# The border between the mixer and the cross-attention: first weights begun before the second token tile's norm, low parts of the query weights in other places, two groups' wide products in a row

## The chip, the cores and the metric

The kernel runs on one core of one Trainium2 chip. Times are device microseconds (us) of one execution; a kernel's time is the median of several runs. The engines named below are PE (TensorE: matmuls, with PEld for its weight loads), DVE (VectorE: elementwise work, 32x32 block transposes), ACT (ScalarE: copies, casts, activations), POOL (GpSimd) and SP (SyncE, which here only issues DMAs).

## What is computed

Two layers, each of four blocks with a residual sum and a layer norm: a SwiGLU, the mixer, the cross-attention, a second SwiGLU. 256 tokens of width 1024, 256 memory rows, everything in float32. What matters here is the end of the mixer and the start of the cross-attention:

```python
def layer_norm(x, g, b):
    xf = x.astype(jnp.float32)
    mu = jnp.mean(xf, axis=-1, keepdims=True)
    var = jnp.mean(jnp.square(xf - mu), axis=-1, keepdims=True)
    return ((xf - mu) * lax.rsqrt(var + LN_EPS)).astype(x.dtype) * g + b
...
    q = (x @ wq).reshape(bsz, s, CA_HEADS, CA_HEAD_DIM)
    k = (mem @ wk).reshape(bsz, m, CA_HEADS, CA_HEAD_DIM)
    v = (mem @ wv).reshape(bsz, m, CA_HEADS, CA_HEAD_DIM)
...
        mix = jnp.concatenate([y_conv, y_rec, y_pool], axis=-1) @ w_out[l]
        h = layer_norm(ALPHA * h + mix, ln_g[l, 1], ln_b[l, 1])
        h = layer_norm(ALPHA * h + cross_attn(h, mem, ca_q[l], ca_k[l], ca_v[l], ca_o[l]),
                       ln_g[l, 2], ln_b[l, 2])
```

The values (`mem @ wv`) don't depend on the norm; the queries (`x @ wq`) need all of it.

## The kernel before

**Split numbers.** Each matmul operand is held as a rounded high part and a low part. `split` (L74 to L77) makes them: ACT casts the high part (L75), DVE subtracts it from the source (L76, recorded in the list `lows`). A product is high times high, high times low and low times high. In `mm_cols`, which forms 128 output columns for all 256 tokens, a *wide* product takes one high 128x128 block of a weight against a token block with high and low part side by side (512 columns), and a *narrow* one takes the low block of the weight against the high part alone (256 columns). It issues seven wide products, eight narrow ones and the last wide one, into one PSUM bank. Weights of 512 columns come in four tiles of two row blocks each: so product k of a chain needs tile k // 2.

**Weights.** `load` issues the DMAs on SP into `raw` tiles (6 buffers), and splits them into `whi` and `wlo` tiles (8 buffers of each). With `hold` it only lists the splits in `todo`, and the caller issues them.

**Tokens.** They lie in two tiles of 128, `h[0]` and `h[1]`. `project_back` multiplies the mixer's output with `w_out` in four slabs of two row blocks; the last three slabs are run for one token tile and column half at a time (`tail`), so that each tile can be normed as soon as its sums are done. `finish` norms: `tile_done(i)` adds the sums to `h[i]` (L378), makes the mean (DVE, L388), the square on ACT (L393), the variance (DVE, L399), its power on POOL (L405) and two more DVE passes (L408, L413, the latter recorded in `normed`).

**The border.** With `across` set (this border alone), after `tile_done(0)` four DMAs on POOL's queue deal `h[0]` out to the tile `dealt` (L424), `tile_done(1)` follows, and two DVE transposes (L433) make `turned` from `dealt`: the first tile's tokens, turned. In `attention`, `values` loads `ca_v` (512 columns) and forms the values of the memory rows; these products, 24 for each of two row tiles, keep PE busy while the norm ends. Within the second row tile's products, `first_rows` splits `turned` into `xT` (before k = 0), and `pend` turns the second token tile with eight PE transposes into two PSUM banks and splits these into the other half of `xT` (before k = 4). Then `query(0)` loads `ca_q` and forms the queries of two heads in two pairs of column groups; `query(1)` does so for the next columns. Banks: `acc` tiles have four PSUM banks in common, and the values' two sums, the two turned banks and the queries' sums all come from these four.

**Order.** Tile's planner sets the order on each engine at build time, from the order in the program and its own estimate of what is ready when; it fills an engine's wait with later work that is ready. `with tc.issue_after(ins)` puts what a block issues on the engine of `ins` behind `ins`, and does nothing on the other engines. Before the change, `ca_q`'s low parts for both halves were put behind the last norm pass in this way (`normed[-1]`). Once built, the list of each engine is fixed.

Of the kernel before, what the change touches and what calls it, by code (L numbers as in the profile page):

```python
# [17 lines left out]
P = 128  # L18
# [42 lines left out]
def model(ctx: ExitStack, tc: tile.TileContext, t: dict, out: bass.AP):  # L61
# [79 lines left out]
    def mm_cols(w, cols, x):  # L141
        o = acc()
        for k in range(NK - 1):
            product(o, w.at(k, cols)[0], x[:, k], k == 0, False)
        for k in range(NK):
            product(o[:, 0, :], w.at(k, cols)[1], x[:, k, 0, :], False, False)
        product(o, w.at(NK - 1, cols)[0], x[:, NK - 1], False, True)
        return sums(o)

    def add(dst, o):  # L150
        dst = dst if len(dst.shape) == 3 else halves(dst)
# [177 lines left out]
    def finish(mm, y, scale, gb, units, last=False, junk=None, ahead=None, prompt=False, across=None):  # L329
# [25 lines left out]
        def tile_done(i):  # L355

            st = sm.tile([P, 4, 6], F32, tag="st", name="st")
            pieces, size = [slice(0, 512), slice(512, DM)], 512
            if last and i == NT - 1:

                pieces, size = [slice(0, 512), slice(512, 768), slice(768, DM)], 256
                c = slice(512, DM)
                v = halves(h[i][:, c])
                with tc.issue_after(lows[-1].ins):
                    nc.vector.scalar_tensor_tensor(v, v, ALPHA / scale, sums(y[i][1]), op0=ALU.mult, op1=ALU.add)
            for c in pieces:
                n = c.start // 512
                v = halves(h[i][:, c])
                if len(pieces) == 3 and n:
                    o = acc((P, 256))  # L370
                    mm(i, n, slice(c.start - 512, c.stop - 512), o, None)
                    nc.vector.tensor_tensor(v, v, sums(o), op=ALU.add)
                else:
                    mm(
                        i, n, slice(0, 512), None,
                        None if last or across or not i or not n else turn_first,
                    )
                    nc.vector.scalar_tensor_tensor(  # L378
                        v, v, ALPHA / scale, sums(y[i][n]), op0=ALU.mult, op1=ALU.add,
                        accum_out=None if junk is None else st[:, n, 0:1],  # L380
                    )
                for d in range(c.start, c.stop, size):
                    if junk is None:
                        nc.vector.bn_stats(st[:, d // size, :], h[i][:, d : d + size])
            mv = sm.tile([P, 2], F32, tag="mv", name="mv")
            rs = sm.tile([P, 1], F32, tag="rs", name="rs")
            if junk is not None:
                mean = nc.vector.tensor_scalar(  # L388
                    mv[:, 0:1], st[:, 0, 0:1], st[:, 1, 0:1], -1.0 / DM, op0=ALU.add, op1=ALU.mult
                )  # L390
                with ExitStack() as behind:
                    squared.append(
                        nc.scalar.activation(junk, h[i], AF.Square, bias=mv[:, 0:1], accum_out=mv[:, 1:2])  # L393
                    )
                    if prompt:
                        with tc.issue_after(mean.ins):
                            low_part(held.pop(0))
                        behind.enter_context(tc.issue_after(lows[-1].ins))
                    nc.vector.tensor_scalar(  # L399
                        rs, mv[:, 1:2], 1.0 / DM, LN_EPS / scale / scale, op0=ALU.mult, op1=ALU.add  # L400
                    )
            else:
                nc.vector.bn_aggr(mv, st[:, 0 : DM // size, :])
                nc.vector.tensor_scalar_add(rs, mv[:, 1:2], LN_EPS / scale / scale)
            nc.gpsimd.tensor_tensor(rs, rs, nhalf[:, 0:1], op=ALU.pow)  # L405
            cs = [slice(0, 512), slice(512, DM)]
            for c in cs:
                nc.vector.scalar_tensor_tensor(  # L408
                    h[i][:, c], h[i][:, c], mv[:, 0:1], g[:, c],
                    op0=ALU.subtract if junk is None else ALU.add, op1=ALU.mult,  # L410
                )
            for c in pieces:
                normed.append(nc.vector.scalar_tensor_tensor(  # L413
                    h[i][:, c], h[i][:, c], rs, b[:, c], op0=ALU.mult, op1=ALU.add
                ))
                if last:
                    e = nc.scalar if c.start == 512 else nc.sync
                    e.dma_start(out[0, tok(i), c], h[i][:, c])

        if across is not None:  # L420
            tile_done(0)
            x = across()
            for a in range(4):
                dealt = nc.gpsimd.dma_start(  # L424
                    x[a * 32 : a * 32 + 32].rearrange("p (b c) -> p b c", b=4), h[0][:, a * 256 : (a + 1) * 256]
                )
            with tc.issue_after(dealt.ins):
                tile_done(1)
            o = wp.tile([P, DM], F32, tag="lng", name="turned").rearrange("p (k t) -> p k t", k=NK)
            m = x.rearrange("p (b j k) -> p k b j", b=4, k=NK)  # L430
            with tc.issue_after(normed[-1].ins):
                for d in (slice(0, 4), slice(4, 8)):
                    nc.vector.transpose(o[:, d].rearrange("p k (r b) -> p k b r", b=4), m[:, d])  # L433
            firsts.append(o)
        elif ahead is None:
            tile_done(0)
            tile_done(1)
        else:
            split(*ahead.todo[0])
            if prompt:  # L440
                nc.scalar.copy(ahead.todo[1][0], ahead.todo[1][2])
                held.append(ahead.todo[1])
            with tc.issue_after(lows[-1].ins):
                tile_done(0)
            with tc.issue_after(normed[-1].ins):
                if prompt:
                    split(*ahead.todo[2])
                    split(*ahead.todo[3])
                tile_done(1)
                if not prompt:  # L450
                    for x in ahead.todo[1:]:
                        split(*x)
            if prompt:
                with tc.issue_after(normed[-1].ins):
                    low_part(held.pop())
# [500 lines left out]
            d = slice(4 * c + 2 * p, 4 * c + 2 * p + 2)  # L956
            split(kTh[:, d, :], kTl[:, d, :], o)

    def values(l, c, vh, vl, between={}):
        w = load(t["ca_v"][l], 0, NK, c * CHUNK, CHUNK, across=True)  # L960
        for i in range(NT):
            o = acc((P, 512))
            for k in range(NK):
                if k % 2 == 0:
                    between.get(4 * i + k // 2, lambda: None)()
                wh, wl = w.at(k, slice(0, CHUNK))
                mm_rows(o, mT[:, k, 0, tok(i)], mT[:, k, 1, tok(i)], wh, wl, k == 0, k == NK - 1)
            d = slice(c * CHUNK, (c + 1) * CHUNK)
            split(halves(vh[:, i, d]), halves(vl[:, i, d]), sums(o))

    def mixer(l, fill):
        w_in = t["w_in"][l]
        with tc.tile_pool(name="mix", bufs=1, reuse_waits="tile") as mp:

# [336 lines left out]
            def slab(a):  # L1313
# [2 lines left out]
            return project_back(  # L1316
                [slab(a) for a in (0, 6, 2, 4)], 3, gb, 1.0, idn,
                junk=v.rearrange("p i c -> p (i c)"),
                across=lambda: mp.tile([P, DM], F32, tag="q", name="dealt"),
            )  # L1320


    def attention(l, pend):
        scale = (DM // HEADS) ** -0.5
        with tc.tile_pool(name="att", bufs=1, reuse_waits="tile") as ap:
            qTh = ap.tile([P, NK, SEQ], F32R, name="qTh")
# [4 lines left out]

            def query(c, between=None):

                with tc.issue_after(normed[-1].ins):
                    w = load(t["ca_q"][l], 0, NK, c * CHUNK, CHUNK, across=True)
                for p in range(2):
                    o = sm.tile([P, 2, SEQ], F32, tag="sums", name="sums", bufs=1)
                    for j in range(2):
                        add(o[:, j, :], mm_cols(w, slice((2 * p + j) * P, (2 * p + j + 1) * P), xT))
                    d = slice(4 * c + 2 * p, 4 * c + 2 * p + 2)  # L1340
                    split(qTh[:, d, :], qTl[:, d, :], o)
                    if between is not None and p == 0:
                        between()
# [68 lines left out]

            def first_rows():
                for d in (slice(0, 4), slice(4, 8)):
                    split(xTh[:, d, tok(0)], xTl[:, d, tok(0)], firsts[-1][:, d])

            pT = []
            values(l, 0, vh, vl, {4: first_rows, 6: pend})
            query(0)
            gb = ln_params(l, 2)  # L1420
            query(1, lambda: (weights(0), deal(0), weights(1), deal(1)))
# [25 lines left out]
    for l in range(DEPTH):  # L1447
# [2 lines left out]
            following=(lambda: key_weights(l, 0, True)) if l else None,  # L1450
        )
        keys(l, 0, {6: pend}, started)
        pend = mixer(l, lambda: keys(l, 1))
        pend = attention(l, pend)
        end = l == DEPTH - 1
        started, pend = ffn(
            l, "ffn2", 3, pend, last=end,
# [29 lines left out]
```

## Time and profile before

| | |
|---|---|
| median of 3 runs (lowest, highest) | 1065.58 us (1065.34, 1065.7) |
| the profiled execution, its own time | 1064.91 us |
| its span, first to last instruction | 1063.2 us |
| PE busy / DVE busy / ACT busy / POOL busy | 99% / 88% / 63% / 9% of the span |
| granted TensorE clock, mean | 0.999 |
| instructions | 16487 |

The border is passed twice, once in each layer: at about 281 to 306 us and at about 805 to 830 us of the span. In the rows of the timeline, the first two numbers are start and length in us, then come engine, line, operation, what is written from what, and the count of instructions merged in the row; brackets at the end hold the engine's idle time before the row and what ended it. The length of a merged row reaches from its first start to its last end.

### The profile page before, as it was taken

The page shows a single profiled execution, that of the slowest core. Times are in us where ns is not written, and L with a number is a line of the kernel's source. Part 1 is how long each engine was busy: PE and PEld are TensorE (multiplying, and loading weights), DVE is VectorE, ACT ScalarE, POOL GpSimd, SP SyncE. Part 2 cuts the span into 40 slices and gives each one's busy share as a digit, 9 for nine tenths or more (in the row PEclk, how much of TensorE's full clock was granted, in tenths as well). Part 3 has the DMA queues.
Part 4 walks back from the last instruction along what each step waited for, and adds up shares of the span by engine and source line. Part 5 has one row for each costly group of instructions (what it writes and reads, how often), then busy time and mean ns, then how long its engine had stood idle before and what let it go on. Part 6 is the DMA issues. An engine that isn't in the chain of part 4 may idle for free.

```text
span 1063.2 us, 16487 instructions
## 1 busy us (share of the span) xinstructions
PE 1050.1 (99%) x5998; PEld 932.8 (88%) x5998; DVE 932.6 (88%) x1250; ACT 666.8 (63%) x917; POOL 99.6 (9%) x136
## 2 busy tenths in 40 slices
PE   9999999999999999999999999999999999999997
PEld 7888888989889888889888888898998898888896
DVE  6998898989899789897898987999898887898888
ACT  6675775676657557655665656666775665675661
POOL 8002001000100001010001001010001000000001
PEclk9999999999999999999999999999999999999999
DMA  9999984754775589988789987866636765799862
GB/s 362 298 318 281 262 267 164 254 166 150 228 249 193 168 283 231 358 200 215 242 304 258 337 226 203 271 232 221 209 117 212 258 234 173 242 283 310 234 201 70
DMA packets 142689, 252.11 MB, mean 237 GB/s; under 512 B 11376, under 2 KB 52112, under 8 KB 142608
## 3 DMA queue, kind: packets, MB, share of 16 engines
q1 hardware_dynamic: 130656, 228.89, 65.0%
q0 software_dynamic: 11376, 20.99, 11.1%
q10 hardware_dynamic: 576, 1.18, 0.3%
q8 instruction: 47, 0.77, 0.3%
q14 instruction: 34, 0.28, 0.1%
HBM read 234.50 MB, written 1.05 MB: 222 GB/s over the span
## 4 chain that ended last, share of the span: by engine, by line
PE 92%; DVE 4%; DMA 1%; issue 1%; ACT 1%; POOL 0%; DVEq 0%; ACTq 0%; POOLq 0%; SPq 0%
PE acc L132 61%; PE dn L132 28%; DVE wlo L76 2%; ACT whi L75 1%; PE acc L200 1%; DMA h<-in_x_dram 1%; DMA dealt<-h 1%; DVE turned L433 0%; PE dn L1155 0%; DMA raw<-in_ca_q_dram 0%; PE dn L1229 0%; DVE h L413 0%; DVE raw L718 0%; DVE h L408 0%; DVE al L76 0%
## 5 line engine op out<-in xcount | busy, mean ns | idle before, releaser
L76 DVE TENSOR_TENSOR wlo<-raw,whi 128x1024 fp32r<-128x1024 f32 (+1 forms) x452 | 534.3, 1209 | 51.9 <-ACT whi L75 47.2
L75 ACT CAST whi<-raw 128x1024 fp32r<-128x1024 f32 (+1 forms) x452 | 455.9, 1042 | 186.8 <-PE acc L132 47.0
L132 PE MATMUL acc<-whi,xT 128*128 128x512 f32 (+1 forms) x1064 | 313.7, 372 | 0.0
L132 PEld LDWEIGHTS acc<-whi,xT 128*128 128x128 f32 x1064 | 199.1, 189 | 26.7
L132 PE MATMUL acc<-wlo,xT 128*128 128x512 f32 (+1 forms) x532 | 197.9, 372 | 0.0
L132 PE MATMUL dn<-whi,ah 128*128 128x512 f32 x346 | 131.5, 380 | 0.0
L132 PE MATMUL dn<-wlo,ah 128*128 128x512 f32 x346 | 131.2, 379 | 0.1
L132 PE MATMUL dn<-whi,al 128*128 128x512 f32 x346 | 131.1, 379 | 0.0
L132 PE MATMUL acc<-xT,whi 128*128 128x512 f32 x480 | 118.2, 382 | 3.3 <-DVE xT L76 3.3
L132 PEld LDWEIGHTS acc<-wlo,xT 128*128 128x128 f32 x532 | 100.6, 189 | 13.3
L132 PEld LDWEIGHTS acc<-xT,whi 128*128 128x128 f32 x480 | 86.5, 190 | 13.6 <-DVE xT L76 4.1
L132 PE MATMUL dn<-whi,xT 128*128 128x512 f32 x288 | 87.3, 380 | 0.0
L132 PEld LDWEIGHTS dn<-wlo,ah 128*128 128x128 f32 x346 | 65.4, 189 | 9.4 <-DVE wlo L76 0.5
L132 PEld LDWEIGHTS dn<-whi,al 128*128 128x128 f32 x346 | 65.4, 189 | 9.3
L132 PEld LDWEIGHTS dn<-whi,ah 128*128 128x128 f32 x346 | 65.4, 189 | 9.0
L132 PEld LDWEIGHTS acc<-xT,wlo 128*128 128x128 f32 x480 | 63.1, 191 | 4.1 <-DVE wlo L76 0.9
L132 PE MATMUL acc<-xT,wlo 128*128 128x256 f32 x480 | 63.8, 275 | 0.1
L132 PE MATMUL acc<-wlo,kTh 128*128 128x512 f32 (+1 forms) x176 | 61.7, 351 | 0.0
L132 PE MATMUL acc<-whi,kTl 128*128 128x512 f32 (+1 forms) x176 | 61.7, 351 | 0.0
L132 PE MATMUL acc<-whi,kTh 128*128 128x512 f32 (+1 forms) x176 | 61.7, 351 | 0.0
L132 PEld LDWEIGHTS dn<-whi,xT 128*128 128x128 f32 x288 | 54.4, 189 | 7.7 <-DVE xT L76 0.2
L132 PE MATMUL dn<-wlo,xT 128*128 128x512 f32 x144 | 54.6, 379 | 0.0
(258 smaller groups left out, 1301.2 us busy)
## 6 DMA issues: line engine op xcount, KB each, us to landing
raw<-in_ffn_up_dram SPq DMA_DIRECT2D x88, 512.0 KB, 5.7
raw<-in_ffn_down_dram SPq DMA_DIRECT2D x88, 512.0 KB, 5.8
raw<-in_ffn_gate_dram SPq DMA_DIRECT2D x84, 512.0 KB, 5.5
raw<-in_w_in_dram SPq DMA_DIRECT2D x48, 512.0 KB, 4.5
dealt<-sg SPq DMA_DIRECT2D x80, 128.0 KB, 5.0
raw<-in_ffn_up_dram POOLq DMA_DIRECT2D x19, 512.0 KB, 6.1
raw<-in_ffn_gate_dram POOLq DMA_DIRECT2D x16, 512.0 KB, 9.6
raw<-in_ca_k_dram SPq DMA_DIRECT2D x16, 512.0 KB, 5.3
```

The lines of the kernel that those rows point to most:

```text
L75: rounded = nc.scalar.copy(hi, src)
L76: lows.append(nc.vector.tensor_tensor(lo, src, hi.bitcast(F32), op=ALU.subtract))
L132: turns.append(nc.tensor.matmul(o, w, x, start=start, stop=stop, skip_group_check=more))
L200: turns.append(nc.tensor.transpose(pt[:, k % 4, :], x, unit))
```

## The change

`finish` now calls a function `begin` of its caller right after the four deal DMAs, and so before `tile_done(1)`: it loads the first values' weights (split at once, as before) and the first query weights (held). Of the held splits, the first one's cast is issued there, with `tile_done(1)`'s ACT work behind it; its low part is issued by `tile_done(1)` after the mean, and the variance step is put behind it. The second one is split after the transposes (its cast behind the square). The third and the fourth are split after the values, their low parts behind the last low part of `pend`. `values` hands its own two splits back, and `attention` issues them after that, their low parts behind the fourth one's. `query(0)` forms its first two column groups with a new function `mm_two`: the seven wide products of both groups, then for each group its eight narrow ones and the last wide one. `query(1)`'s weights are no longer put behind the norm. `dealt` is allocated before `project_back` is called.

```diff
+    def mm_two(w, cols, x):
+        o = [acc() for _ in cols]
+        for n, c in enumerate(cols):
+            for k in range(NK - 1):
+                product(o[n], w.at(k, c)[0], x[:, k], k == 0, False)
+        for n, c in enumerate(cols):
+            for k in range(NK):
+                product(o[n][:, 0, :], w.at(k, c)[1], x[:, k, 0, :], False, False)
+            product(o[n], w.at(NK - 1, c)[0], x[:, NK - 1], False, True)
+        return [sums(x) for x in o]
...
-                    if prompt:
+                    if prompt or across is not None and i:
                         with tc.issue_after(mean.ins):
                             low_part(held.pop(0))
                         behind.enter_context(tc.issue_after(lows[-1].ins))
...
             tile_done(0)
-            x = across()
+            x, begin = across
             for a in range(4):
                 dealt = nc.gpsimd.dma_start(
                     x[a * 32 : a * 32 + 32].rearrange("p (b c) -> p b c", b=4), h[0][:, a * 256 : (a + 1) * 256]
                 )
-            with tc.issue_after(dealt.ins):
+            w = begin()
+            held.append(w.todo[0])
+            cast = nc.scalar.copy(w.todo[0][0], w.todo[0][2])
+            with tc.issue_after(dealt.ins), tc.issue_after(cast.ins):
                 tile_done(1)
...
                 for d in (slice(0, 4), slice(4, 8)):
-                    nc.vector.transpose(o[:, d].rearrange("p k (r b) -> p k b r", b=4), m[:, d])
-            firsts.append(o)
+                    turned = nc.vector.transpose(o[:, d].rearrange("p k (r b) -> p k b r", b=4), m[:, d])
+            with tc.issue_after(turned.ins), tc.issue_after(squared[-1].ins):
+                split(*w.todo[1])
+            firsts.append((o, w))
...
-    def values(l, c, vh, vl, between={}):
-        w = load(t["ca_v"][l], 0, NK, c * CHUNK, CHUNK, across=True)
+    def values(l, c, vh, vl, between={}, started=None):
+        w = started or value_weights(l, c)
+        held = []
...
-            split(halves(vh[:, i, d]), halves(vl[:, i, d]), sums(o))
+            held.append((halves(vh[:, i, d]), halves(vl[:, i, d]), sums(o)))
+            if started is None:
+                split(*held.pop())
+        return held
...
-                with tc.issue_after(normed[-1].ins):
-                    w = load(t["ca_q"][l], 0, NK, c * CHUNK, CHUNK, across=True)
+                w = first_query if not c else query_weights(l, c)
...
+                    if c or p:
+                        for j in range(2):
+                            add(o[:, j, :], mm_cols(w, cols[j], xT))
+                    else:
+                        for j, x in enumerate(mm_two(w, cols, xT)):
+                            add(o[:, j, :], x)
...
-            values(l, 0, vh, vl, {4: first_rows, 6: pend})
+            made = values(l, 0, vh, vl, {4: first_rows, 6: pend}, first_values)
+            with tc.issue_after(lows[-1].ins):
+                for x in first_query.todo[2:]:
+                    split(*x)
+            with tc.issue_after(lows[-1].ins):
+                for x in made:
+                    split(*x)
...
+        def begin():
+            begun.append(value_weights(l, 0))
+            begun.append(query_weights(l, 0, True))
+            return begun[1]
+
+        pend = mixer(l, lambda: keys(l, 1), begin)
+        pend = attention(l, pend, *begun)
```

More of the change, by code (lines that the diff above doesn't have):

```diff
@@ L968, in values, with mixer @@
             d = slice(c * CHUNK, (c + 1) * CHUNK)
-            split(halves(vh[:, i, d]), halves(vl[:, i, d]), sums(o))
-    def mixer(l, fill):
+            held.append((halves(vh[:, i, d]), halves(vl[:, i, d]), sums(o)))
+            if started is None:
+                split(*held.pop())
+        return held
+    def mixer(l, fill, begin):
         w_in = t["w_in"][l]
@@ L1318, in mixer, with value_weights, query_weights, attention @@
                 junk=v.rearrange("p i c -> p (i c)"),
-                across=lambda: mp.tile([P, DM], F32, tag="q", name="dealt"),
+                across=(mp.tile([P, DM], F32, tag="q", name="dealt"), begin),
             )
-    def attention(l, pend):
+    def value_weights(l, c):
+        return load(t["ca_v"][l], 0, NK, c * CHUNK, CHUNK, across=True)
+    def query_weights(l, c, hold=False):
+        return load(t["ca_q"][l], 0, NK, c * CHUNK, CHUNK, across=True, hold=hold)
+    def attention(l, pend, first_values, first_query):
         scale = (DM // HEADS) ** -0.5
@@ L1332, in query @@
             def query(c, between=None):
-                with tc.issue_after(normed[-1].ins):
-                    w = load(t["ca_q"][l], 0, NK, c * CHUNK, CHUNK, across=True)
+                w = first_query if not c else query_weights(l, c)
                 for p in range(2):
                     o = sm.tile([P, 2, SEQ], F32, tag="sums", name="sums", bufs=1)
-                    for j in range(2):
-                        add(o[:, j, :], mm_cols(w, slice((2 * p + j) * P, (2 * p + j + 1) * P), xT))
+                    cols = [slice((2 * p + j) * P, (2 * p + j + 1) * P) for j in range(2)]
+                    if c or p:
[4 more added lines that the diff above has]
+                            add(o[:, j, :], x)
                     d = slice(4 * c + 2 * p, 4 * c + 2 * p + 2)
@@ L1414, in first_rows @@
                 for d in (slice(0, 4), slice(4, 8)):
-                    split(xTh[:, d, tok(0)], xTl[:, d, tok(0)], firsts[-1][:, d])
+                    split(xTh[:, d, tok(0)], xTl[:, d, tok(0)], firsts[-1][0][:, d])
             pT = []
-            values(l, 0, vh, vl, {4: first_rows, 6: pend})
+            made = values(l, 0, vh, vl, {4: first_rows, 6: pend}, first_values)
[5 more added lines that the diff above has]
+                    split(*x)
             query(0)
@@ L1452, in model @@
         keys(l, 0, {6: pend}, started)
-        pend = mixer(l, lambda: keys(l, 1))
-        pend = attention(l, pend)
+        begun = []
+        def begin():
[4 more added lines that the diff above has]
+        pend = attention(l, pend, *begun)
         end = l == DEPTH - 1
```

## The prediction

> **What bounds the kernel now.** I read the page first (busy times, chain of waits), then who waited for whom on PE, then the timeline of each engine around the two borders.
>
> ```profile
> PE 1050.1 (99%) x5998; PEld 932.8 (88%) x5998; DVE 932.6 (88%) x1250; ACT 666.8 (63%) x917; POOL 99.6 (9%) x136
> PE 92%; DVE 4%; DMA 1%; issue 1%; ACT 1%; POOL 0%; DVEq 0%; ACTq 0%; POOLq 0%; SPq 0%
> ...
> PE acc L132 <- DVE xT L76: 3.3, 2, 1.6
> PE dn L578 <- DVE kTh L573: 1.5, 1, 1.5
> PE acc L597 <- DMA h<-in_x_dram: 0.6, 1, 0.6
> ```
>
> PE is busy 99% of the span and leads 92% of the chain that ended last. So work saved elsewhere is worth nothing unless PE waits for it, and PE's own list of waits has three entries. The first one, twice 1.6 us, is the wait for `xT` at this border, once in each layer. Its size on PE's own timeline, layer 0 and then layer 1:
>
> ```profile
> 299.47 0.38 PE L132 MATMUL acc<-whi,mT 128*128 128x512 f32 x1
> 301.47 1.78 PE L132 MATMUL acc<-xT,whi 128*128 128x512 f32 x7 [1.62 <-DVE xT L76]
> 303.08 0.83 PE L132 MATMUL acc<-xT,wlo 128*128 128x256 f32 x6
> 303.75 1.25 PE L132 MATMUL acc<-xT,whi 128*128 128x512 f32 x5
> 305.02 0.49 PE L132 MATMUL acc<-xT,wlo 128*128 128x256 f32 x2
> ...
> 823.75 0.38 PE L132 MATMUL acc<-whi,mT 128*128 128x512 f32 x1
> 825.76 1.78 PE L132 MATMUL acc<-xT,whi 128*128 128x512 f32 x7 [1.63 <-DVE xT L76]
> ...
> 828.04 1.25 PE L132 MATMUL acc<-xT,whi 128*128 128x512 f32 x5
> 829.36 0.49 PE L132 MATMUL acc<-xT,wlo 128*128 128x256 f32 x2
> ```
>
> Wide products follow each other every 0.217 us (five in 1.25, the last taking 0.38: 0.87 / 4), narrow ones every 0.11 (six from 303.08 to 303.75). The last values product starts at 299.47, so the first query product could start at 299.69; it starts at 301.47: **1.78 us lost**. After the five wide products from 303.75 the next could start at 304.83 and starts at 305.02: 0.19 lost, for a low part. Layer 1 loses 825.76 - 823.97 = 1.79 and 829.36 - 829.12 = 0.24. Together **4.00 us** are in reach (0.38%); no part of the change can give more, as it takes no product away.
>
> **What makes `xT` late.** DVE's timeline in layer 0:
>
> ```profile
> 289.49 0.21 DVE L388 TENSOR_SCALAR mv<-st 128x1 f32<-128x1 f32 x1
> 291.42 0.15 DVE L399 TENSOR_SCALAR rs<-mv 128x1 f32<-128x1 f32 x1 [1.71 <-ACT v L393]
> ...
> 294.13 2.70 DVE L433 STREAM_TRANSPOSE turned<-dealt 128x512 f32<-128x512 f32 x2
> 296.64 1.24 DVE L76 TENSOR_TENSOR wlo<-raw,whi 128x1024 fp32r<-128x1024 f32 x1
> 297.78 0.70 DVE L76 TENSOR_TENSOR vl<-acc,vh 128x512 fp32r<-128x512 f32 x1
> 298.37 1.30 DVE L76 TENSOR_TENSOR xT<-turned,xT 128x512 fp32r<-128x512 f32 x2
> 299.56 1.25 DVE L76 TENSOR_TENSOR wlo<-raw,whi 128x1024 fp32r<-128x1024 f32 x1
> 300.69 1.32 DVE L76 TENSOR_TENSOR xT<-acc,xT 128x512 fp32r<-128x512 f32 x2
> ...
> 303.14 0.69 DVE L76 TENSOR_TENSOR vl<-acc,vh 128x512 fp32r<-128x512 f32 x1
> 303.75 3.48 DVE L76 TENSOR_TENSOR wlo<-raw,whi 128x1024 fp32r<-128x1024 f32 x3
> ```
>
> From the transposes at 294.13 on DVE has no idle time; between them and `pend`'s first low part at 300.69 stand two low parts of query weights (1.14 and 1.13 us from start to next start) and one of the values (0.59). PE starts 0.78 after `pend`'s first low part does (300.69 to 301.47). ACT is the second candidate:
>
> ```profile
> 285.41 4.83 ACT L75 CAST whi<-raw 128x1024 fp32r<-128x1024 f32 x5 [2.31 <-PE dn L132]
> 290.15 1.15 ACT L393 ACTIVATE v<-h,mv 128x1024 f32<-128x1024 f32 x1
> 291.29 1.03 ACT L75 CAST whi<-raw 128x1024 fp32r<-128x1024 f32 x1
> 295.70 0.63 ACT L75 CAST xT<-turned 128x512 fp32r<-128x512 f32 x1 [3.38 <-DVE turned L433]
> 296.86 0.62 ACT L75 CAST xT<-turned 128x512 fp32r<-128x512 f32 x1
> 297.39 1.99 ACT L75 CAST whi<-raw 128x1024 fp32r<-128x1024 f32 x2
> 299.28 1.06 ACT L75 CAST xT<-acc 128x512 fp32r<-128x512 f32 x2
> ...
> 296.22 1.04 PE L200 MATMUL acc<-idn,h 128*128 128x128 f32 x8
> ```
>
> The transposes of the second tile are off PE at 297.26, but their casts start at 299.28: the planner put two weight casts ahead (297.39, 1.99 us). Counting tiles, the six casts from 285.41 to 292.32 are the values' last two and the query's four, so these two belong to `query(1)`. It seems that the planner expected the transposes later than they came, and filled.
>
> **The change, part by part (layer 0; layer 1 has the same steps 524.3 us on).**
>
> *Low part 0 into the norm.* DVE idles from 289.70 to 291.42 while ACT squares. A 1.13 us step behind the mean ends at about 290.85, before the square does: 0 on the path. Without that cover (a late cast 0) it would delay the variance by up to 1.13; the cast is the third of the five from 285.41, over at about 288.3, so it holds. It frees 1.14 us after the transposes, and a `raw` buffer seven us earlier.
>
> *Cast 1 behind the square.* Cast 3 or 2 takes its place among the five; cast 1 then runs from 291.29, hidden by ACT's wait up to 295.70 (3.38 us idle). The square itself stays behind five casts: 0. If only four go ahead, it starts at about 289.75 instead of 290.15 and everything behind moves 0.4 up.
>
> *Low part 1 behind the transposes:* 296.64 to 297.78, as one low part is there now: 0.
>
> *Low parts 2, 3 and both values' low parts behind `pend`:* takes 0.59 and, by the program, 1.13 out of the way. What is late next: low parts 2 and 3 themselves (about 2.3 us behind `pend`'s second) and the values' banks.
>
> *`mm_two`:* 16 wide and 16 narrow products as before. The first narrow one comes 14 x 0.217 = 3.04 us after the start instead of 1.5; low part 2 is due after four of them (3.48), low part 3 after six (3.70). `pend`'s second low part ends 1.2 - 0.78 = 0.42 after PE's start, so low parts 2 and 3 are done at 1.55 and 2.7: in time. So the stalls of 0.19 and 0.24 go.
>
> *Loads begun earlier.* The eight DMAs (four for values, four for queries) come earlier in the program, ahead of `tile_done(1)`, but SP holds them until `raw` buffers come free, which the same low parts decide:
>
> ```profile
> 287.74 1.50 SPq L101 DMA_DIRECT2D raw<-in_ca_q_dram  x2
> 294.25 0.34 SPq L323 DMA_DIRECT2D lnb<-in_ln_b_dram  x1
> ...
> 300.00:312.00 12.00, 10.51 (x62) 9.33 (x63) 11.11 (x14) 5.70 (x10) 0.00 (x0) 1.00 0.87 305
> ...
> 653.58 1.07 ACT whi L75
> ...
> 688.43 7.17 PE dn L132 x32
> ```
>
> I give this step 0. Between is `lnb`, which waits on SP for the last norm pass (its buffer) with two `query(1)` loads queued behind; POOL's four deal DMAs keep their place.
>
> *What is left of the stall.* This is the unknown. If DVE alone decided: transposes to 296.64, low part 1 to 297.78, two `xT` low parts to 298.97 (1.19), then `pend`: PE at 298.97 + 0.78 = 299.75, a stall of 0.06. But two hold-ups are not removed. First, the two `query(1)` casts on ACT: `pend`'s first cast ends 299.28 + 0.53, its low part starts about 299.87, PE 300.65: stall 0.96. Second, `query(1)`'s low parts: nothing puts them behind `pend`, their first cast is done at 298.34, and before the change the planner filled this same place (299.56) with a low part that was ready. With one of them in it: 298.97 + 1.13 + 0.78 = 300.88, stall 1.19. The lower bound is 0.06, the upper one is the third case below. As both hold-ups are in the rows now, I take the middle of 0.96 and 1.19, 1.08.
>
> **Sum.** 4.00 - 2 x 1.08 = 1.85 us. The profiled execution's own 1064.91 (span 1063.2 and 1.7 around it) becomes 1063.06; it lies 0.67 under the median, so against the median 1065.58 - 1.85 = **1063.7**. That layer 0's share reaches the end is likely: PE has no wait behind the border but one of 1.5 at L578 and short ones for weights; in the one long stretch where the chain runs over DVE (653.58 to 688.43 in the chain), it begins with a cast that PE's progress releases.
>
> **The cases.** A measurement of this kernel can tell about 0.2% (2.1 us) from no change.
>
> 1. *Half of the stall goes*, as above: 1063.5 to 1064.0, or 1062.7 where the square also starts 0.4 earlier in both layers. Chance 0.37, of which 0.07 beyond 0.2%.
>
> 2. *All of it goes*: the planner casts `pend`'s banks at once, and no `query(1)` low part comes first. 4.00 - 2 x 0.06 = 3.9: **1061.7**. For it: with two 1.1 us fillers and the values' low part gone, DVE and ACT have room, and PE's list shows no wait for `xT` at any other border. Against it: the two casts at 297.39. Chance 0.32.
>
> 3. *The wait is refilled*: DVE takes two `query(1)` low parts before `pend`, since its estimate has `pend` late. 298.97 + 2.26 + 0.78 = 302.01, stall 2.32: 2 x 2.32 - 4.00 = +0.6, **1066.2**, no difference that counts. For it: the casts of both would be over at 299.28, before `pend`'s. Against it: before, one filler sufficed until `pend` was taken. Chance 0.16.
>
> 4. *Slower: no bank for the second group.* The values' two sums now hold two of the four `acc` banks until their low parts, behind low parts 2 and 3: 301.3 (end of `pend` at a start of 300.88) + 2.27 + 0.6 = 304.2, PE 304.35. If `mm_two`'s second group gets such a bank, PE, due there at 300.88 + 1.52 = 302.40, waits 1.95: with 1.19, 3.14 a layer, 2 x 3.14 - 4.00 = +2.3, **1067.9**. If already the first one does, the stall is 4.66 and the time 1065.6 + 2 x 4.66 - 4.00 = 1070.9. It decides from the moment that one of the two groups isn't given the banks of `pend`. Against it: before, the second group's wide products began at 303.75, before the values' second low part ended (303.14 + 0.69), so it held a bank other than that one. Chance 0.15.
>
> The Trainium skill, page "TensorE: Matmul & The Clock Gate", section "Why this matters for your kernels", has the matmul clock drop to half after idle gaps over about 3 us. By it only case 4's longer stall would cost more, some 1.7 us a layer (an estimate: one window of 3.4 us at half speed); with today's 1.6 us the granted clock stayed 1.00 in the 12 us behind (300 to 312), which agrees.
>
> **Range and chances.** 1061.4 to 1066.4 holds cases 1 to 3, 0.85; the likeliest case alone spans 1062.7 to 1064.3. Faster by over 0.2%: case 2 and 0.07 of case 1, 0.39. Slower by over 0.2%: case 4 and 0.01 of case 3, 0.16. Within: 0.45.
>
> **What will show it.** Right: a low part of weights between mean and variance on DVE; no values' low part before `pend`'s; PE's first query row at 300.6 to 300.9 (less whatever moved before) with two casts, or one weight low part, still ahead of `pend`'s; 14 wide query products in a row without a gap to the narrow ones. Case 2 shows `pend`'s casts directly behind the transposes, case 3 two weight low parts before `pend`'s, case 4 a gap after seven wide products, or a start behind `vl`. Wrong would also be a square later than 290.15, or a new wait in PE's list further down.

## The result and the profile after

| | before | after |
|---|---|---|
| median (lowest, highest), 21 runs each | 1065.54 us (1065.09, 1067.07) | 1064.18 us (1063.37, 1065.37) |
| after / before, 95% interval | | 0.9986 [0.9979, 0.9992] |
| span of the profiled execution | 1063.2 us | 1061.7 us |

The change takes off 1.36 us, with an interval of 0.9 to 2.2 us (0.08% to 0.21% of 1065.54): a small gain, inside what was called no difference that counts. The predicted gain was 1.85 us.

The page after: busy times of the engines, chain of waits, and then PE's list of waits (engine, line and releaser; us in total, times, longest).

```profile
PE 1049.2 (99%) x5998; PEld 932.9 (88%) x5998; DVE 932.3 (88%) x1250; ACT 665.8 (63%) x917; POOL 99.6 (9%) x136
PE 98%; DMA 1%; DVE 0%; ACT 0%; issue 0%; ACTq 0%; DVEq 0%
PE acc L132 <- DVE xT L76: 2.1, 2, 1.0
PE dn L594 <- DVE kTh L589: 1.5, 1, 1.5
PE acc L613 <- DMA h<-in_x_dram: 0.8, 2, 0.5
```

The wait for `xT` shrank from 3.3 to 2.1 us and is still the first entry; DVE's 4% of the chain is gone. PE's timeline at the two borders:

```profile
299.35 0.38 PE L132 MATMUL acc<-whi,mT 128*128 128x512 f32 x1
300.76 3.29 PE L132 MATMUL acc<-xT,whi 128*128 128x512 f32 x14 [1.02 <-DVE xT L76]
303.88 1.05 PE L132 MATMUL acc<-xT,wlo 128*128 128x256 f32 x8
...
822.40 0.38 PE L132 MATMUL acc<-whi,mT 128*128 128x512 f32 x1
823.82 3.29 PE L132 MATMUL acc<-xT,whi 128*128 128x512 f32 x14 [1.04 <-DVE xT L76]
```

The stall before the first query product is 300.76 - 299.35 - 0.217 = 1.19 us in layer 0 and 1.20 in layer 1 (it was 1.78 and 1.79). Fourteen wide products run in one row and eight narrow ones follow in one row: the waits of 0.19 and 0.24 for low parts are gone. Of 4.00 us, 2.39 are left. What makes `xT` late now, on ACT and then on DVE:

```profile
287.18 1.04 ACT L440 CAST whi<-raw 128x1024 fp32r<-128x1024 f32 x1
289.67 1.15 ACT L404 ACTIVATE v<-h,mv 128x1024 f32<-128x1024 f32 x1 [1.45 <-DVE mv L399]
...
296.50 0.62 ACT L75 CAST xT<-turned 128x512 fp32r<-128x512 f32 x1 [0.60 <-DVE turned L447]
297.02 0.58 ACT L75 CAST vh<-acc 128x512 fp32r<-128x512 f32 x1
297.50 1.99 ACT L75 CAST whi<-raw 128x1024 fp32r<-128x1024 f32 x2
299.39 1.07 ACT L75 CAST xT<-acc 128x512 fp32r<-128x512 f32 x2
```

```profile
289.36 0.21 DVE L399 TENSOR_SCALAR mv<-st 128x1 f32<-128x1 f32 x1
289.49 1.21 DVE L362 TENSOR_TENSOR wlo<-raw,whi 128x1024 fp32r<-128x1024 f32 x1
290.94 0.15 DVE L410 TENSOR_SCALAR rs<-mv 128x1 f32<-128x1 f32 x1 [0.24 <-ACT v L404]
...
296.30 1.21 DVE L76 TENSOR_TENSOR wlo<-raw,whi 128x1024 fp32r<-128x1024 f32 x1
297.44 1.26 DVE L76 TENSOR_TENSOR xT<-turned,xT 128x512 fp32r<-128x512 f32 x2
300.01 1.29 DVE L76 TENSOR_TENSOR xT<-acc,xT 128x512 fp32r<-128x512 f32 x2 [1.31 <-ACT xT L75]
...
303.48 1.28 DVE L76 TENSOR_TENSOR vl<-acc,vh 128x512 fp32r<-128x512 f32 x2
```

DVE has what it needs done at 298.7 and then idles for 1.31 us; no low part of `query(1)` was put into that gap. It waits for ACT, whose queue runs one values' cast and the two weight casts of `query(1)` (297.02 to 299.39), while the turned banks lie ready from 297.14 on (PE's eight transposes start at 296.09 and take 1.05). So the engine that decides has changed: DVE before, ACT's order after.

Of the 1.61 us that PE gained at the borders not all arrives. From the issue of the last output DMA on SP to the end of the span it was 1063.2 - 1060.0 = 3.2 us before, and it is 1061.7 - 1057.7 = 4.0 after. The view of the output tile, of before and then of after (count, shortest, median and longest length in ns, first and last start in us):

```profile
L418 SPq DMA_DIRECT2D out_dram<-h x3: 332/352/354, 1051.8 to 1060.0; - x3
```

```profile
L429 SPq DMA_DIRECT2D out_dram<-h x3: 332/344/354, 1049.5 to 1057.7; - x3
```

### The profile page after: what moved, and what is told of

Read it like the earlier page. It is cut to its first block, busy times and chain, and to the rows that moved or that the text cites. A ratio compares the mean times of both kernels' runs of the same rounds, so it can differ in the third digit from the quotient of the medians.

```text
span 1061.7 us, 16488 instructions
## 1 busy us (share of the span) xinstructions
PE 1049.2 (99%) x5998; PEld 932.9 (88%) x5998; DVE 932.3 (88%) x1250; ACT 665.8 (63%) x917; POOL 99.6 (9%) x136
## 3 DMA queue, kind: packets, MB, share of 16 engines
HBM read 234.50 MB, written 1.05 MB: 222 GB/s over the span
## 4 chain that ended last, share of the span: by engine, by line
PE 98%; DMA 1%; DVE 0%; ACT 0%; issue 0%; ACTq 0%; DVEq 0%
PE acc L132 65%; PE dn L132 31%; PE acc L211 1%; DMA h<-in_x_dram 1%; PE dn L1175 0%; PE dn L1249 0%; ACT whi L75 0%; PE dn L1248 0%; PE dn L1237 0%; PE acc L1317 0%; DVE xT L76 0%; PE dn L1200 0%; DVE h L424 0%; PE acc L613 0%; ACT xT L75 0%
## 5 line engine op out<-in xcount | busy, mean ns | idle before, releaser
L76 DVE TENSOR_TENSOR wlo<-raw,whi 128x1024 fp32r<-128x1024 f32 (+1 forms) x450 | 531.1, 1208 | 49.9 <-ACT whi L75 44.8
```

The lines of the kernel that those rows point to most:

```text
L76: lows.append(nc.vector.tensor_tensor(lo, src, hi.bitcast(F32), op=ALU.subtract))
```

## The experiments

**Two theories.** A: ACT's order sets the start (casts put ahead of `pend`'s), and with these out of the way the stall ends. B: DVE sets it, and what helps is every low part that is moved out of `xT`'s way. Each kernel below changes one thing. "Border" is the sum of PE's waits at the two borders, read from each kernel's PE timeline as above; "later" is what PE waits between 685 and 690 us, in the last part of layer 1's first feed-forward.

| kernel | border, us | later, us | median, us | before beside it, us | ratio, 95% interval |
|---|---|---|---|---|---|
| before (first profile) | 4.00 | 0.24 | 1065.54 | | |
| after | 2.39 | 0 | 1064.18 | 1065.54 | 0.9986 [0.9979, 0.9992] |
| x1 | 0 | 0.60 | 1062.80 | 1065.66 | 0.9969 [0.9956, 0.9981] |
| x2 | 4.04 | 0.41 | 1065.88 | 1065.66 | 1.0002 [0.9993, 1.0011] |
| x3 | 2.43 | 0.59 | 1064.90 | 1065.66 | 0.9996 [0.9987, 1.0004] |
| x4 | 1.89 | 0.92 | 1064.51 | 1065.66 | 0.9986 [0.9978, 0.9995] |
| x5 | 3.60 | 0.48 | 1065.75 | 1065.76 | 0.9999 [0.9990, 1.0008] |
| x6 | 2.32 | 0.54 | 1064.81 | 1065.76 | 0.9990 [0.9981, 0.9999] |
| x7 | 2.91 | 0.47 | 1064.75 | 1065.76 | 0.9989 [0.9981, 0.9998] |
| x8 | 0 | 0 | 1061.86 | 1065.76 | 0.9962 [0.9949, 0.9974] |
| y1 (before again) | 4.31 | 0.25 | 1065.47 | 1065.56 | 0.9999 [0.9990, 1.0008] |
| y2 (after again) | 2.42 | 0 | 1064.17 | 1065.56 | 0.9985 [0.9976, 0.9994] |
| y3 (x1 again) | 0 | 0.44 | 1062.30 | 1065.56 | 0.9969 [0.9958, 0.9980] |
| y4 (x8 again) | 0 | 0.18 | 1061.17 | 1065.56 | 0.9961 [0.9948, 0.9975] |

Kernels x1 to x4, x5 to x8 and y1 to y4 ran together, each group on a chip of its own with the kernel before beside it; where a kernel is set against after below, the two medians come from different groups, among which before moved by 0.2 us. Most differences between neighbours in the table are smaller than their intervals; it is the waits in the traces that tell them apart, and the medians that show how much of them counts.

### x1: the casts of `query(1)` behind `pend`'s

```diff
         rounded = nc.scalar.copy(hi, src)
+        highs.append(rounded)
...
-                w = first_query if not c else query_weights(l, c)
+                with tc.issue_after(after_pend.ins):
+                    w = first_query if not c else query_weights(l, c)
...
             made = values(l, 0, vh, vl, {4: first_rows, 6: pend}, first_values)
+            after_pend = highs[-1]
```

> After the change PE still waits 1.19 and 1.20 us at the two borders. Theory A (ACT): pend's two casts stand behind one values cast and two query(1) casts. With query(1)'s casts behind pend's, pend's first cast starts at about 297.5 instead of 299.4, its low part at 298.6 (DVE free), PE at about 299.4, before the values end: the stall falls to under 0.15 at each border, the time by about 2.2 to 2.4 us against the changed kernel, to 1061.8. Theory B (DVE's low parts, or the banks, set the start): no more than 0.3 us.

In x1, the values' cast still comes first on ACT, but the weight casts no longer; below are x1's ACT, DVE and PE (lines behind L76 are one higher than in after).

```profile
297.03 0.58 ACT L75 CAST vh<-acc 128x512 fp32r<-128x512 f32 x1
297.51 1.08 ACT L75 CAST xT<-acc 128x512 fp32r<-128x512 f32 x2
```

```profile
297.42 1.29 DVE L77 TENSOR_TENSOR xT<-turned,xT 128x512 fp32r<-128x512 f32 x2
298.60 1.31 DVE L77 TENSOR_TENSOR xT<-acc,xT 128x512 fp32r<-128x512 f32 x2
```

```profile
299.33 0.38 PE L133 MATMUL acc<-whi,mT 128*128 128x512 f32 x1
299.55 3.18 PE L133 MATMUL acc<-xT,whi 128*128 128x512 f32 x14
...
822.24 3.19 PE L133 MATMUL acc<-xT,whi 128*128 128x512 f32 x14
```

PE goes from the values to the queries without a gap, in both layers: the two casts were the whole stall, and theory A holds. DVE's row shows how narrow it is: `pend`'s first low part starts at 298.60, 0.95 before PE; in after PE followed it by 0.75, so 0.2 us are to spare. The time, 1062.8, falls 1.0 short of the 1061.8 that the borders alone would give. Part of the missing us is in the trace, at the end of layer 1's first feed-forward, where DVE now stands 0.92 us for a dealing DMA and PE then 0.60 for DVE:

```profile
683.03 0.77 DVE L564 STREAM_TRANSPOSE square<-dealt 128x256 f32<-128x256 f32 x2 [0.92 <-DMA dealt<-both]
```

That DMA, the slowest of the deal's four, took 5.5 us to land here and 5.31 in the repeat (y3). A second wait of this kind, of 1042.74 - 1042.15 - 0.217 = 0.38 us, stands in layer 1's second feed-forward and not in the repeat:

```profile
1042.74 0.48 PE L133 MATMUL dn<-wlo,ah 128*128 128x512 f32 x1 [0.21 <-DVE wlo L77]
```

A further 0.35 us lies outside the span (see behind y4).

### x2: the same gate on the kernel before

```diff
-                with tc.issue_after(normed[-1].ins):
+                with tc.issue_after(normed[-1].ins), tc.issue_after((marks if c else normed)[-1].ins):
                     w = load(t["ca_q"][l], 0, NK, c * CHUNK, CHUNK, across=True)
```

(`marks` holds `pend`'s last cast.)

> The kernel before, with query(1)'s casts behind pend's: the one part that the change lacks, alone. Theory A+B (two limits, one behind the other): pend's first low part comes at about 299.6, PE starts at 300.3 instead of 301.5, but DVE was without a break from 294 to 305, so the query's fourth low part still ends at 304.9 and PE waits there instead (0.7 to 0.8 before the third, 0.5 to 0.6 before the fourth): time within 0.5 us of the kernel before. Rival (ACT's order alone is the matter, the change's moves of low parts are not needed): about 2.2 us less than before, 1063.3.

x2's PE timeline, layer 0:

```profile
300.34 1.78 PE L133 MATMUL acc<-xT,whi 128*128 128x512 f32 x7 [0.53 <-DVE xT L77]
...
303.20 0.49 PE L133 MATMUL acc<-xT,wlo 128*128 128x256 f32 x2 [0.63 <-DVE wlo L77]
...
305.17 0.49 PE L133 MATMUL acc<-xT,wlo 128*128 128x256 f32 x2 [0.41 <-DVE wlo L77]
```

The first wait falls from 1.78 to 0.69 us. At the narrow products a new wait of 0.80 us appears, and the one that was 0.19 before grows to 0.57, because PE now arrives sooner and the weights' low parts are late: 2.06 instead of 1.97, as expected. ACT's order alone is worth nothing where DVE has too much to do; the change's moves on DVE are what makes the gate in x1 worth anything. The reverse holds in part as well: after, with the change's moves and no gate, gets 1.61 of the 4.00.

### x3 and x4: low part 0 back behind the transposes, without and with the gate

```diff
-                    if prompt or across is not None and i:
+                    if prompt:
...
             with tc.issue_after(turned.ins), tc.issue_after(squared[-1].ins):
+                low_part(held.pop())
                 split(*w.todo[1])
```

> The changed kernel with low part 0 behind the transposes again, not between mean and variance. Theory A: DVE idles 1.31 us before pend's low parts, which covers the 1.14: no change, within 0.3 us of the changed kernel (1064.2). Theory B: pend's low parts move 1.14 back at each border, 2.3 us slower, 1066.5.

> Both: query(1)'s casts behind pend's, and low part 0 behind the transposes. Theory A: the cover of x3 is gone, DVE sets the start: pend's low part at about 299.8, PE at 300.5, stall 0.95 a border: 1.9 us slower than x1, about 1063.7. Rival (low part 0's place is worth nothing anywhere): as x1.

x3's DVE and PE and, below them, x4's DVE and PE:

```profile
297.39 1.20 DVE L76 TENSOR_TENSOR wlo<-raw,whi 128x1024 fp32r<-128x1024 f32 x1
298.51 1.26 DVE L76 TENSOR_TENSOR xT<-turned,xT 128x512 fp32r<-128x512 f32 x2
299.95 1.29 DVE L76 TENSOR_TENSOR xT<-acc,xT 128x512 fp32r<-128x512 f32 x2 [0.18 <-ACT xT L75]
```

```profile
300.70 3.29 PE L132 MATMUL acc<-xT,whi 128*128 128x512 f32 x14 [1.03 <-DVE xT L76]
```

```profile
300.56 1.27 DVE L77 TENSOR_TENSOR xT<-acc,xT 128x512 fp32r<-128x512 f32 x2
```

```profile
301.29 3.29 PE L133 MATMUL acc<-xT,whi 128*128 128x512 f32 x14 [0.77 <-DVE xT L77]
```

In x3 two low parts of weights stand behind the transposes and not one. The extra 1.14 us on DVE fits into the 1.31 us for which it waited anyway: 0.18 of that is left, and PE's stall is 1.19 and 1.24 as in after. So in the kernel as changed, the moved low part 0 gains nothing at this border. The time was expected within 0.3 us of after and is 0.7 above it; the border has no part in that, but the late wait (0.59, none in after) and 0.35 us outside the span have. In x4, with ACT's casts out of the way, the same low part costs 0.93 and 0.96 us, since DVE now has no idle time between the transposes and `pend`. The expected stall was 0.95; the time, 1064.5 and not 1063.7, has 0.92 us of late waits on top. The move is a precondition of a gain that the change itself doesn't reach.

### x5: without `mm_two`

```diff
-                    if c or p:
-                        for j in range(2):
-                            add(o[:, j, :], mm_cols(w, cols[j], xT))
-                    else:
-                        for j, x in enumerate(mm_two(w, cols, xT)):
-                            add(o[:, j, :], x)
+                    for j in range(2):
+                        add(o[:, j, :], mm_cols(w, cols[j], xT))
```

> The changed kernel with the first two column groups one after the other (seven wide, eight narrow, one wide each). All other engines keep their order up to the first sums. PE starts as in the changed kernel (stall 1.2) and reaches the narrow product k = 6 of the first group 2.2 us later, at 302.95; low part 3 is done at about 303.6: a new wait of about 0.65 a border, 1.3 us slower than the changed kernel, 1065.5. If the low parts were not late: no change.

```profile
301.84 1.78 PE L132 MATMUL acc<-xT,whi 128*128 128x512 f32 x7 [1.08 <-DVE xT L76]
303.46 0.83 PE L132 MATMUL acc<-xT,wlo 128*128 128x256 f32 x6
304.70 0.49 PE L132 MATMUL acc<-xT,wlo 128*128 128x256 f32 x2 [0.42 <-DVE wlo L76]
```

The first stall stays (1.24 and 1.20) and low part 3 makes PE wait 0.58 in each layer; the gain is gone (0.9999). `mm_two` is worth 0.58 a border, more than the 0.19 and 0.24 that stood in the trace of before, since the change also moved low parts 2 and 3 back.

### x6: the values' low parts at once

```diff
-            if started is None:
-                split(*held.pop())
+            split(*held.pop())
```

> The changed kernel with the values' two splits issued at once, as before the change. The values' cast moves ahead of xT's second cast, into ACT's idle time, so pend's casts come 0.48 earlier and PE starts at about 300.3 (stall 0.75 instead of 1.2); but the second values' low part stands before low parts 2 and 3, and PE waits about 0.45 for low part 3: together no change within 0.4 us (1064.2). If holding the values back were worth its 0.6 us on DVE: 1.2 us slower.

x6's ACT and PE:

```profile
296.44 0.58 ACT L75 CAST vh<-acc 128x512 fp32r<-128x512 f32 x1
297.20 0.62 ACT L75 CAST xT<-turned 128x512 fp32r<-128x512 f32 x1 [0.17 <-DVE turned L447]
```

```profile
300.98 3.29 PE L132 MATMUL acc<-xT,whi 128*128 128x512 f32 x14 [0.61 <-DVE xT L76]
...
305.16 0.49 PE L132 MATMUL acc<-xT,wlo 128*128 128x256 f32 x2 [0.23 <-DVE wlo L76]
```

Here the planner puts the values' cast into ACT's wait for the second transpose, where it costs nothing, and not behind it. The queries start 0.41 sooner (stall 0.78) and then wait 0.39 for low part 3, behind the values' low parts on DVE. Border 2.32 against 2.39: holding the values back moved a wait and removed none. Both waits came as expected; the time, 0.6 above after instead of within 0.4, again holds a late wait (0.54) and 0.35 us outside the span.

### x7: two more casts ahead of the square

```diff
-            cast = nc.scalar.copy(w.todo[0][0], w.todo[0][2])
+            for n in (0, 2, 3):
+                cast = nc.scalar.copy(w.todo[n][0], w.todo[n][2])
```

(Of splits 2 and 3 only the low parts are left for later.)

> The changed kernel with casts 2 and 3 ahead of the square, as my prediction took the order to be. The square starts at about 290.03 instead of 289.67 in the changed kernel, and everything behind moves by as much: stall 1.55 a border, 0.7 us slower, 1064.9. If the square's place does not matter: no change.

```profile
287.27 2.93 ACT L441 CAST whi<-raw 128x1024 fp32r<-128x1024 f32 x3
290.11 1.14 ACT L404 ACTIVATE v<-h,mv 128x1024 f32<-128x1024 f32 x1
```

```profile
299.44 0.38 PE L132 MATMUL acc<-whi,mT 128*128 128x512 f32 x1
301.11 3.29 PE L132 MATMUL acc<-xT,whi 128*128 128x512 f32 x14 [1.29 <-DVE xT L76]
```

This puts five casts before the square, as they were before the change. The square starts at 290.11 (289.67 in after), and the stall grows from 1.19 and 1.20 to 1.45 and 1.46. So the change gained 0.26 a border by having only three casts there. Its text puts cast 0 ahead of the square and leaves casts 2 and 3 to the planner, which put them behind it.

### x8: the values' casts behind `pend`'s as well

x1, and:

```diff
-            with tc.issue_after(lows[-1].ins):
+            with tc.issue_after(lows[-1].ins), tc.issue_after(after_pend.ins):
                 for x in made:
                     split(*x)
```

> As x1, with the values' casts behind pend's too. In x1 DVE is the later of the two (xT's own low parts end at 298.6, pend's first cast at 298.0), so the values' cast in between (0.48) costs nothing: the time of x1 within 0.3 us. If ACT still sets the start in x1: up to 1 us faster than x1.

x8's list of PE's waits, then its timeline on ACT, on PE and, at the late deal's place, on DVE:

```profile
PE dn L595 <- DVE kTh L590: 1.5, 1, 1.5
PE acc L614 <- DMA h<-in_x_dram: 0.6, 1, 0.6
```

```profile
297.17 1.07 ACT L75 CAST xT<-acc 128x512 fp32r<-128x512 f32 x2
```

```profile
299.66 3.18 PE L133 MATMUL acc<-xT,whi 128*128 128x512 f32 x14
...
821.50 3.19 PE L133 MATMUL acc<-xT,whi 128*128 128x512 f32 x14
```

```profile
682.07 0.77 DVE L564 STREAM_TRANSPOSE square<-dealt 128x256 f32<-128x256 f32 x2
```

No wait at either border, none at 685 to 690 us (the transpose of the deal didn't have to wait), and a time of 1061.86, the fastest of all: 3.9 us below before, and 2.3 below after, where after's borders had 2.39. It was expected within 0.3 us of x1 and is 0.9 below. PE's list keeps two entries that this border has nothing to do with.

### y1 to y4: before, after, x1 and x8 once more, together

> The kernel before, unchanged, on the same chip as the next three. Open after the first runs: behind PE's last product the changed kernel's profile takes 8.4 us to the end of the span, that of the kernel before 7.7, because the last output DMAs land in 2.7 us instead of 2.05. If that belongs to the kernel: 2.0 to 2.1 here again. If it is chance: anything from 2.0 to 3.0. Time 1065.5 within 0.3.

> The changed kernel, unchanged. If the late landing belongs to the kernel: output DMAs 2.6 to 3.0 us again. PE's waits at the border 1.2 us each again, the wait at the end of layer 1's first feed-forward block between 0 and 0.6 us as its deal DMA lands in 4.9 to 5.6 us. Time 1064.2 within 0.4.

> x1 again. x1 and x8 have the same order on PE and DVE and no wait at the border, yet x8 was 0.9 us faster. Theory A: the border is done in both, and the 0.9 us is the landing of one deal DMA (5.5 us in x1's profile, 4.7 in x8's), which varies: the two agree within 0.5 us here, near 1062.3. Rival: the values' cast ahead of pend's costs x1 its 0.5 us a border: x1 0.9 us above x8 again.

> x8 again, for the same question. Theory A: within 0.5 us of y3. Rival: 0.9 us below y3. Against the kernel before 3.3 to 3.9 us less.

The four medians repeat within 0.7 us: 1065.47, 1064.17, 1062.30, 1061.17. So x8 is again the fastest, by 4.4 us against before (0.9961), and again ahead of x1, by 1.1 us (0.9 the first time): both expectations of "within 0.5 us" and "within 0.3 us" missed, and of the twelve runs of x1 and y3 seven are slower than the slowest of the ten of x8 and y4 (1062.23). The two kernels differ in ACT's order alone, in their traces too, and neither has a wait at a border, so the rival, a cost of the values' cast at the border, isn't what happened either.

A third of the gap lies outside the span. Every run's time is longer than its span from first to last instruction: by 2.01 to 2.12 us in all runs of x1, y3, x3 and x6, and by 1.66 to 1.78 in all runs of the other kernels. What these 0.35 us are, no trace shows.

The rest lies inside, at places that change. Between the two query starts x1 takes 0.85 us longer than x8 (822.24 - 299.55 = 522.69 against 821.50 - 299.66 = 521.84), of which 0.60 is the late deal; behind the second start it takes 1.1 longer, with the wait at 1042.74 and a longer end. In y3 and y4, 0.5 us come ahead of the first border (300.02 against 299.51), 0.3 between the two starts and none behind. The late deal is in both pairs, but its landing alone doesn't tell them apart: in y4 the DMA took 5.35 us to land, as long as in y3, and PE waited only 0.18 and not 0.44. DVE's transpose starts 0.53 us after the last landing in y3 (682.69 to 683.22) and 0.2 in y4 (682.2 to 682.39). Why x1 should meet these waits more often stays open.

The profiles also speak on the end of the run. From the start of the last output DMA to the end of the span it is 3.2 us in before, in y1 (1060.7 to 1063.9) and in x2, and 3.9 to 4.3 us in after, in y2 (1059.6 to 1063.5) and in the nine other profiles of kernels that hold the change. So it belongs to the program and isn't chance. x3, x5 and x6 each take back one part of the change (low part 0's place, `mm_two`, the held values), x7 puts five casts before the square again, and all four keep the longer end; so none of these alone makes it.

## Why the prediction came out as it did

The likeliest case came true: half of the stall goes, 1063.7 forecast, 1064.18 measured. But some of the steps were wrong, and two of them worked against each other, so that the number came this close is in part luck.

**The size of what is left.** Forecast: 1.08 us a border, the middle of 0.96 (two casts of `query(1)` ahead of `pend`'s on ACT) and 1.19 (one low part of `query(1)` ahead of `pend`'s on DVE). Measured: 1.19 and 1.20, but not for the second reason. That hold-up did not occur; DVE sat idle in the place where it was expected. The first one did, and its 0.96 was too small by 0.23: `pend`'s low part started at 300.01 and not 299.87, since the held-back values' cast (0.48 from start to next start) was put ahead of the two weight casts, and the values' last product started at 299.35 and not 299.47 (0.14 + 0.12, less 0.03 as PE followed the low part by 0.75 and not 0.78). x1 shows ACT's casts to be the whole stall. Against the 1.08 that was taken it is 0.11 and 0.12 more, 0.23 us over both borders.

**The step of the values.** "Both values' low parts behind `pend`" was said to free 0.59 on DVE. It did, on an engine that no longer decided. What was overlooked is that a split is two instructions: its cast moved with it, into the way of `pend`'s casts on ACT. x6 gives the price: nothing gained.

**The square.** Forecast at 0 behind five casts, or 0.4 earlier behind four. It stood behind three and started 0.48 earlier (290.15 to 289.67), held now by the mean on DVE and no longer by casts (ACT idles 1.45 us before it); x7 prices that at 0.26 a border. Without this gain the stall would have been 1.45, and the sum would have come out at about 1.1 us (4.00 - 2.91).

**Low part 0 in the norm, low part 1.** Hidden, as said: low part 0 ends at 290.70 and the variance step starts at 290.94, waiting for the square; low part 1 stands behind the transposes (296.30). That it "frees 1.14 us" is true of DVE only; x3 shows no gain in PE's start.

**`mm_two`.** Right: 14 wide products, no gap, no wait for low parts 2 and 3, and banks for both groups at once. x5 shows that it was needed (0.58 a border). The slower case, a missing bank, did not occur.

**Loads begun earlier.** Forecast at 0, and so it came: SP issues the values' loads from 269.06 on (269.19 before) and the queries' from 274.88 on (275.00 before): 0.12 to 0.13 sooner, as much as the values' last product. They weren't tried alone.

**All of it goes.** This case had 0.32. The change doesn't reach it; x1 and x8 do with the mechanism named there, `pend`'s banks cast early, and x8 with the time too: 1061.86 and 1061.17 against the forecast of 1061.7. The counter-argument, the two casts at 297.39, was the right one.

**From PE to the end.** The borders gave 1.61 us, and PE's wait of 0.24 near 688 us went too, together 1.85, as many as forecast by chance. With 0.1 us behind each of the three waits that went (first point of the last section) and 0.12 ahead of the first border, PE is 2.27 us sooner at its last product. The step that failed is that all of it reaches the end: the profiled spans differ by 1.53 although the last output DMA was issued 2.3 us earlier, for about 0.75 us were lost behind the last product. The medians differ by 1.36; with an interval of 0.9 to 2.2 us they cannot tell 1.36 from 1.85 by themselves.

## What to carry to other kernels

Where an engine's order is fixed at build time, an engine that is busy 63% can still set the pace: look at what stands in its queue ahead of the instruction that the bound engine waits for, and put filler behind that instruction by hand. A wait with two causes on two engines pays little until both are gone: ACT's gate alone gave nothing (x2), the change without the gate 1.4 us, both together 2.9 and 3.3 (x1 and y3), and 3.9 and 4.4 with the values' casts out of the way too (x8 and y4; a part of that last step lies outside the borders). And when a step is moved, move all its instructions on paper: the cast that went along with a low part cost what the low part's move was meant to gain.

## What the runs showed of the hardware

- PE's first row behind a wait is about 0.1 us longer than the same row without one: 14 wide products take 3.29 us behind a wait and 3.18 in x1 and x8. So a removed stall is worth 0.1 more than its length.
- The last output DMA takes 0.7 to 1.1 us longer to the end of the span in the eleven profiles of kernels with the change (3.9 to 4.3) than in the three without it (3.2 each), with the same bytes from the same tile. The cause is open.
- One DMA from SBUF to SBUF, the slowest of the deal in layer 1's first feed-forward, landed 4.87 us after its issue in y2, 5.31 in y3 and 5.65 in x4, and PE waited 0, 0.44 and 0.92 us there. A wait of this kind, 390 us behind the border, is as large as most differences in the table.
- Two kernels with the same order of instructions on every engine but ACT differ by 0.35 us in the time outside their span, in every run (x1: 2.02 to 2.12, x8: 1.66 to 1.75). So a difference of this size between two medians need not be a wait in the trace.
